# A two-layer hybrid trunk: gelu stores from ScalarE, key products ahead of the heads, a third gate buffer

## The chip, the cores and the metric

The kernel runs on one core of a Trainium2 chip. The metric is the time of one execution in microseconds of device time; of several runs the median counts. All arrays are float32, with batch 1, 1024 positions and a width of 1024.

## The reference

Only the first of the two layers is touched by the change. It computes, from `h = rmsnorm(x, norm_g[0])`:

```python
def mixer_ab(h, w_in, ..., glu_w, glu_b, w_out):
    proj = h @ w_in
    u_s5, g_s5, q, k, v, g_ret = jnp.split(proj, cuts, axis=-1)
    y_s5 = s5_mixer(u_s5, ..., glu_w, glu_b)           # ends with the two lines below
    #   y = jax.nn.gelu(y)
    #   y = y * jax.nn.sigmoid(y @ glu_w + glu_b)
    y_s5 = y_s5 * jax.nn.silu(g_s5)
    y_ret = retention(q, k, v) * jax.nn.silu(g_ret)    # q, k get rotary positions first
    return jnp.concatenate([y_s5, y_ret], axis=-1) @ w_out

def retention(q, k, v):            # 8 heads, 64 wide for q and k, 128 wide for v
    q = rope(q, positions) * (RET_DK ** -0.5)
    k = rope(k, positions)
    scores = einsum('bnihd,bnjhd->bnhij', qc, kc) * intra
    intra_out = einsum('bnhij,bnjhe->bnihe', scores, vc)
    ...                            # states carried from chunk to chunk, normalisation of each head
```

The second layer is a convolution module (projection, a causal convolution of width 31, layer norm, output projection), and a last rmsnorm ends the program.

## The kernel before

All activations lie transposed, features on the 128 partitions and the 1024 positions along the row, in two halves of 512. Every float32 product of the big projections is made as three matmuls (lines 269, 270 and 271, in `mm3`) of operands split into a high and a low part: `wh` and `wl` of the weights, `xh` and `xl` (or `yh` and `yl`, and so on) of the activations. A block of 128 output features is 2 halves x 8 input blocks x 3 = 48 matmuls of 128x512. `wnext` and `wload` bring the weights in a fixed sequence, two blocks ahead of the one in use: a DMA into `wf`, ScalarE's rounded copy `wh`, and the difference `wl` on GpSimd or VectorE (lines 260, 261).

The stages are, in the order of the program: the input projections with the state-space layer (`layer0_front`), the values and heads of the retention (`retention`), and the GLU, the output projection and the whole second layer (`layer0_back_and_layer1`).

The retention runs over four pairs of heads. For each pair `ret_proj` makes the key products (`mm_k`), evacuates them scaled (`kraw`, line 971), and rotates them: four DMAs (line 980) swap halves of partitions into `kswp`, GpSimd multiplies both by the rotary table (lines 984, 986), VectorE adds (line 987) and gives `krot`. Then the same is done for the queries (`mm_q`, `qraw`, `qswp`, `qrot`). `ret_proj` is a generator that yields once between the key products and the rest. Behind it come two calls of `y_pass` (lines 918 to 921), each of which loads one eighth of the state-space output (`yp`, a single buffer), takes the gelu on ScalarE (`yn`, a single buffer) and stores it to `yn_d`. From pair 1 on these follow the last square root of the pair before on ScalarE (`issue_after(self.last_rs.ins)`). Then `ret_heads` does the pair's heads:

- transposes of the keys (`ktp`, line 1077), scaled to `kt` (line 1079),
- the states: `kv` (line 1096) on TensorE and the running sum `S` on VectorE (line 1106),
- the scores `sp` from `krot` and `qrot` (line 1113), masked to `sc` (line 1119),
- the loads of the gates `grl` (line 1128),
- the outputs `ro` (lines 1140, 1145), their statistics on VectorE with a square root on ScalarE (line 540, `rs`), the normalised `on`,
- transposes back (`rt`, line 1168), the product with the gate in place, and the store to `yr_d` (line 1174).

The GLU that follows needs all of gelu(y): `load_split` reads `yn_d` (`yf`, line 1209) and splits it into `yh` and `yl` (lines 1178, 1180), and `mm_glu` sums over all eight blocks of it. Its products read the same operand buffers that hold the input of the query and key products until those are done.

All of the kernel's DMAs are issued by SyncE (SP). The instructions of each engine, SP's DMA issues among them, run in one fixed order. A planner makes that order when the program is built: an instruction that is emitted earlier has the higher priority, and the planner follows the program in a simulated time of its own, in which it takes, on each engine, the instruction of highest priority that is ready by then. `issue_after` and `chained` tie the order of single instructions. A tile with `bufs=n` has n buffers; the next use of a buffer waits for the last reader of the one before.

The key products of the next pair are thus already used as work between the steps of a pair's heads: they come behind the heads in priority, and are taken where the heads are not ready.

Of the kernel before, what the change touches and what calls it, by code (L numbers as in the profile page):

```python
# [11 lines left out]
F32 = mybir.dt.float32  # L12
# [7 lines left out]
P = 128  # L20
D = 1024
T = 1024
# [12 lines left out]
G0 = 3  # L35
TP = 6
LOWS = 18
P_ORDER = ([(1, nb) for nb in range(4)] + [(2, nb) for nb in range(4)] +
           [(i, nb) for i in (6, 7) for nb in range(4)] + [(4, nb) for nb in range(4)])

# [16 lines left out]
class Trunk:  # L57
# [22 lines left out]
    def plan(self):  # L80
# [11 lines left out]
        def wo(*names):  # L92
            return [(None, n) for n in names]

        def ab(h):
            return [q for nb in range(8) for q in ((A["w_c"][8 + nb], f"cb{nb}_{h}"),
                                                   (A["w_c"][nb], f"ca{nb}_{h}"))]
        def cg(h, nbs):
            return [(A["w_c"][16 + nb], f"cg{nb}_{h}") for nb in nbs]
        seq += wo(*(f"p{i}_{nb}" for i, nb in P_ORDER)) + wo("p5_0", "p3_0") + ab(0)  # L100
        seq += wo(*(f"p{i}_{nb}" for nb in range(1, 4) for i in (5, 3)))
# [812 lines left out]
    def y_pass(self, rp, cb):  # L914

        nc = self.nc
        yt = rp.tile([P, 8, P], F32, name=f"yp_{cb}", tag="yp", bufs=1)
        nc.sync.dma_start(yt[:], self.y_d[cb].rearrange("i h g m -> (h g) i m"))
        yn = rp.tile([P, P, 8], F32, name=f"yn_{cb}", tag="ynt", bufs=1)
        nc.scalar.activation(yn[:], yt[:].rearrange("p i m -> p m i"), AF.Gelu_apprx_tanh)  # L920
        nc.sync.dma_start(self.yn_d[cb * P:(cb + 1) * P], yn[:].rearrange("p m i -> p (m i)"))

    def retention(self, st):
        nc, A = self.nc, self.A
        r0 = self.r0 = self.pool("ret0", 1, stack=st)
        early = ExitStack()
        rq = self.rq = self.pool("retq", 1, stack=early, side="right")
        self.vt = [[(r0 if d else rq).tile([P, 4, HALF], F32, name=f"v{d}_{h}") for h in range(2)] for d in range(2)]
        self.rk = rq.tile([P, 2, T], F32, name="ropek")
        nc.sync.dma_start(self.rk[:], A["rope_k"])  # L930
        self.mask = r0.tile([P, NH, P], F32, name="retmask")
        nc.sync.dma_start(self.mask[:], A["ret_mask"])
        self.g128 = r0.tile([P, 4], F32, name="g128")
        nc.sync.dma_start(self.g128[:], A["ret_g128"])
        self.reps = r0.tile([P, NH], F32, name="reteps")
        nc.sync.dma_start(self.reps[:], A["ret_eps"])
        for pair in range(4):
            cur = list(self.ret_proj(pair))[-1]
            if pair == 0:
                with ExitStack() as vst:  # L940
                    V = self.ret_values(self.pool("vp", 1, stack=vst))
                self.rp = self.pool("ret", 1, stack=st)
                self.kdec = self.rp.tile([P, NH, 64], F32, name="kdec")
                nc.sync.dma_start(self.kdec[:], A["ret_kdec"])
                ry = self.pool("rety", 1, stack=early, side="right")
            with ExitStack() as held:
                if pair:
                    held.enter_context(self.tc.issue_after(self.last_rs.ins))
                for cb in (2 * pair, 2 * pair + 1):
                    self.y_pass(ry, cb)  # L950

            def turned():
                if pair == 3:
                    early.close()
                    self.lp = self.pool("l1", side="right")
            self.ret_heads(pair, *cur, V, turned)

    def ret_proj(self, pair):
# [45 lines left out]
    def ret_values(self, vp):  # L1004
# [28 lines left out]
        for n, i in enumerate(V_ORDER):  # L1033
# [29 lines left out]
            with self.tc.issue_after(self.last_sum.ins) if n > 1 else nullcontext():  # L1063
                for k in range(LOWS * (n - 1) // 6, LOWS * n // 6) if n else ():
                    self.weight_low(vp, k, (("wa", "wb"), ("wc", "wd")), 2)
        return lambda p, b, hh: vt[p // 2][b // 4][:, b % 4, (2 * (p % 2) + hh) * P:(2 * (p % 2) + hh + 1) * P]

    def ret_heads(self, pair, K, Q, qadds, V, turned):
        nc, rp = self.nc, self.rp
# [54 lines left out]
        gts = []  # L1124
        for hh in range(2):
            h = 2 * pair + hh
            gt = rp.tile([P, T], F32, name=f"grl_{h}", tag="grl", bufs=2)
            nc.sync.dma_start(gt[:], self.gr_d[h * P:(h + 1) * P])
            gts.append(gt)
        todo = []  # L1130
        for hf in range(2):
# [17 lines left out]
            for hh in range(2):  # L1149
                h, ps = 2 * pair + hh, pss[hh]  # L1150
# [21 lines left out]
        for hh in range(2):  # L1172
            h = 2 * pair + hh
# [8 lines left out]
    def layer0_back_and_layer1(self, st):  # L1182
# [34 lines left out]
        ys0, sg0, t2f, t3f = {}, {}, {}, {}  # L1217
        left = iter(range(LOWS, 32))

# [66 lines left out]
        def w_out_first():  # L1286
            nc.scalar.activation(self.warm[:], self.ones[:, 0:1], AF.Sqrt)
            yr0 = [operand(f"yr0{kb}", "A0", yr_load("yr0f", kb, 0)[:]) for kb in range(KB)]
            m1, u2, u3, t2, t3, t4 = {}, {}, {}, None, None, None
            for i, nb in P_ORDER:  # L1290
                if (i, nb) == (1, 2):
# [460 lines left out]
```

## Time and profile before

| | before |
|---|---|
| median of 3 runs | 1204.38 us (1200.94 to 1206.41) |
| the profiled execution | 1204.63 us |
| its span in the trace | 1202.9 us |
| mean granted TensorE clock | 0.991 |
| TensorE busy with matmuls | 1173.1 us, 98% |
| VectorE, GpSimd, ScalarE busy | 938.3, 688.5, 551.5 us |
| DMA | 271.19 MB, mean 225 GB/s |

The span is the time from the first to the last instruction of the trace. In the lines of the profile PE is TensorE, PEld its weight loads, DVE VectorE, ACT ScalarE, POOL GpSimd, SP SyncE; SPq stands for the issue of DMAs in SP's queue. `A<-B L980` says that tile A is written from B by line 980. An idle time in brackets, `[5.04 <-DVE qrot L987]`, stands ahead of the instruction and names what ended it. Matmuls overlap, so the length of one is longer than the distance to the next.

### The profile page before, as it was taken

Reading aid. Unit: us, or ns where it says so; the run is one execution under the profiler, and the core shown is the slowest. Engines: PE = TensorE matmul, PEld = TensorE weight load, DVE = VectorE, ACT = ScalarE, POOL = GpSimd, SP = SyncE. Lnnn points to the kernel's source line nnn. Section 1 sums busy time; section 2 is a strip of 40 time slices with the busy share of each in tenths; the row PEclk is TensorE's granted clock in tenths of the full one; section 3 lists DMA queues with packets and bytes.
Section 4 is the critical chain, followed back from the end, with each engine's and each line's share of the span. In section 5 each row is a group of like instructions: output and inputs, shape, how many; then the busy total and the mean of one; then the engine's idle time right before and its main releaser. Section 6 shows DMA issues by size and latency. Waiting matters only on the chain.

```text
span 1202.9 us, 17525 instructions
## 1 busy us (share of the span) xinstructions
PE 1173.1 (98%) x6150; PEld 972.4 (81%) x6150; DVE 938.3 (78%) x1529; ACT 551.5 (46%) x831; POOL 688.5 (57%) x489
## 2 busy tenths in 40 slices
PE   9999999999999999988899999999999999999997
PEld 7888888888888878876788788878887887888887
DVE  7865899999518777866878878379999999999643
ACT  7222333333125735323534535267755578444662
POOL 2059989888834224441444033338894578987642
PEclk9999999999999999989999999999999999999999
DMA  9362577788797786656888457866448653356873
GB/s 336 106 194 89 193 270 268 266 282 289 260 303 248 246 274 190 194 175 232 324 288 286 169 211 257 294 235 208 161 152 286 232 179 114 133 186 235 279 253 122
DMA packets 131480, 271.19 MB, mean 225 GB/s; under 512 B 12864, under 2 KB 41792, under 8 KB 131264
## 3 DMA queue, kind: packets, MB, share of 16 engines
q1 hardware_dynamic: 131392, 270.07, 65.8%
q8 instruction: 48, 0.79, 0.3%
q14 instruction: 40, 0.33, 0.1%
HBM read 194.07 MB, written 71.76 MB: 221 GB/s over the span
## 4 chain that ended last, share of the span: by engine, by line
PE 77%; DMA 8%; DVE 8%; issue 2%; POOL 2%; ACT 2%; SPq 1%; DVEq 0%; POOLq 0%; ACTq 0%
PE mm_g L271 7%; PE mm_g L270 7%; PE mm_g L269 6%; PE mm_w L269 4%; PE mm_w L270 4%; PE mm_w L271 4%; PE mm_oc L269 2%; PE mm_oc L270 2%; PE mm_oc L271 2%; PE mm_u L271 2%; PE mm_u L270 2%; PE mm_u L269 2%; PE mm_b L270 2%; PE mm_b L271 2%; PE mm_a L270 2%
## 5 line engine op out<-in xcount | busy, mean ns | idle before, releaser
L1441 DVE SCALAR_TENSOR_TENSOR cv<-u,convw,cv 128x512 f32<-128x512 f32 x358 | 245.2, 747 | 6.0 <-ACT cv L1427 4.3
L1421 POOL TENSOR_TENSOR tp<-tp,tp 128x512 f32<-128x512 f32 x104 | 138.7, 1336 | 33.4 <-ACT tp L1420 27.7
L270 PE MATMUL mm_g<-xl,wh_g 128*128 128x512 f32 x256 | 100.7, 393 | 0.0
L271 PE MATMUL mm_g<-xh,wl_g 128*128 128x512 f32 x256 | 100.7, 393 | 0.0
L269 PE MATMUL mm_g<-xh,wh_g 128*128 128x512 f32 x256 | 100.5, 393 | 0.0
L1420 ACT ACTIVATE tp<-u,convw 128x512 f32<-128x512 f32 x104 | 69.3, 714 | 9.2 <-POOL tp L1421 9.0
L270 PEld LDWEIGHTS mm_g<-xl,wh_g 128*128 128x128 f32 x256 | 48.1, 188 | 11.2 <-issue 1.4
L271 PEld LDWEIGHTS mm_g<-xh,wl_g 128*128 128x128 f32 x256 | 48.1, 188 | 10.4
L269 PEld LDWEIGHTS mm_g<-xh,wh_g 128*128 128x128 f32 x256 | 48.1, 188 | 9.7 <-issue 0.2
L269 PE MATMUL mm_oc<-zh,wh_woc 128*128 128x512 f32 (+1 forms) x152 | 54.5, 362 | 0.0
L271 PE MATMUL mm_oc<-zh,wl_woc 128*128 128x512 f32 (+1 forms) x152 | 54.4, 359 | 0.0
L270 PE MATMUL mm_oc<-zl,wh_woc 128*128 128x512 f32 (+1 forms) x152 | 54.2, 356 | 0.0
L271 PE MATMUL mm_g<-h1h,wl_cg 128*128 128x512 f32 x128 | 50.7, 396 | 1.1 <-POOL wl_cg L261 1.1
L270 PE MATMUL mm_u<-xl,wh_u 128*128 128x512 f32 x128 | 50.0, 391 | 0.9 <-DVE xl L383 0.9
L269 PE MATMUL mm_g<-h1h,wh_cg 128*128 128x512 f32 x128 | 50.9, 397 | 0.0
L269 PE MATMUL mm_glu<-yh,wh_glu 128*128 128x512 f32 x128 | 50.1, 393 | 0.7 <-ACT yh L1178 0.7
L270 PE MATMUL mm_b<-h1l,wh_cb 128*128 128x512 f32 x128 | 50.5, 394 | 0.2 <-DVE h1l L1358 0.2
L270 PE MATMUL mm_g<-h1l,wh_cg 128*128 128x512 f32 x128 | 50.5, 394 | 0.0
L271 PE MATMUL mm_a<-h1h,wl_ca 128*128 128x512 f32 x128 | 50.3, 393 | 0.0
L270 PE MATMUL mm_glu<-yl,wh_glu 128*128 128x512 f32 x128 | 50.1, 391 | 0.2 <-DVE yl L1180 0.2
L269 PE MATMUL mm_b<-h1h,wh_cb 128*128 128x512 f32 x128 | 49.9, 390 | 0.4 <-ACT h1h L1357 0.4
L269 PE MATMUL mm_a<-h1h,wh_ca 128*128 128x512 f32 x128 | 50.1, 392 | 0.0
(812 smaller groups left out, 3634.0 us busy)
## 6 DMA issues: line engine op xcount, KB each, us to landing
wf_g<-w_ab SPq DMA_DIRECT2D x16, 512.0 KB, 4.9
a<-w_out SPq DMA_DIRECT2D x32, 256.0 KB, 4.0
ws<-a SPq DMA_DIRECT2D x32, 256.0 KB, 4.3
lf<-w_c SPq DMA_DIRECT2D x32, 256.0 KB, 4.0
wf_p<-ws SPq DMA_DIRECT2D x16, 512.0 KB, 3.9
wf_cb<-w_c SPq DMA_DIRECT2D x16, 512.0 KB, 4.8
wf_ca<-w_c SPq DMA_DIRECT2D x16, 512.0 KB, 4.7
wl_cb<-lo_cb SPq DMA_DIRECT2D x16, 512.0 KB, 3.3
```

The lines of the kernel that those rows point to most:

```text
L269: nc.tensor.matmul(ps, wh[:, kb, :], xh, start=start, stop=False)
L270: nc.tensor.matmul(ps, wh[:, kb, :], xl, start=False, stop=False)
L271: self.last_mm = nc.tensor.matmul(ps, wl[:, kb, :], xh, start=False, stop=stop)
L1420: nc.scalar.mul(sk[:], u[:, k:k + HALF], cw[:, nb, k:k + 1])
L1421: gp.tensor_tensor(s0[:], s0[:], sk[:], op=ALU.add)
L1441: v.scalar_tensor_tensor(dst[:], *tap, accs_[i][:], op0=ALU.mult, op1=ALU.add)
```

## The change

Three edits in the retention. The DMA that stores gelu(y) is issued by ScalarE, which computed it, and no longer by SP. The key products of pair 1, 2 and 3 are emitted in front of the heads of pair 0, 1 and 2; the rotation of these keys, and the queries, stay behind those heads. The tag of the gates has three buffers, where it had two.

```diff
+AHEAD = (0, 1, 2)
...
         nc.scalar.activation(yn[:], yt[:].rearrange("p i m -> p m i"), AF.Gelu_apprx_tanh)
-        nc.sync.dma_start(self.yn_d[cb * P:(cb + 1) * P], yn[:].rearrange("p m i -> p (m i)"))
+        nc.scalar.dma_start(self.yn_d[cb * P:(cb + 1) * P], yn[:].rearrange("p m i -> p (m i)"))
...
+        ahead = None
         for pair in range(4):
-            cur = list(self.ret_proj(pair))[-1]
+            cur = list(ahead or self.ret_proj(pair))[-1]
...
+            ahead = pair in AHEAD and self.ret_proj(pair + 1)
+            if ahead:
+                next(ahead)
             self.ret_heads(pair, *cur, V, turned)
...
-            gt = rp.tile([P, T], F32, name=f"grl_{h}", tag="grl", bufs=2)
+            gt = rp.tile([P, T], F32, name=f"grl_{h}", tag="grl", bufs=3)
```

## Prediction

> **What bounds the kernel now.** I read the page's engine table first, then the table of stretches for the stage in which the change lies (425 to 600 us, the retention heads), then who waited for whom there, and last the engines' timelines around the two longest waits.
>
> ```profile
> span 1202.9 us, 17525 instructions
> PE 1173.1 (98%) x6150; PEld 972.4 (81%) x6150; DVE 938.3 (78%) x1529; ACT 551.5 (46%) x831; POOL 688.5 (57%) x489
> ```
>
> TensorE (PE) sets the time: it is busy for 1173.1 us of 1202.9. The change neither adds nor removes a matmul, so all it can win is PE's idle time, 29.8 us, and time in which PE ran at a reduced clock. The stretches (length; busy us of PE, PEld, DVE, ACT, POOL; PE clock; DMA share; GB/s) show where these lie:
>
> ```profile
> 495.00:525.00 30.00, 24.96 (x149) 20.86 (x149) 17.31 (x47) 6.96 (x6) 10.32 (x7) 0.94 0.69 207
> 525.00:540.00 15.00, 15.00 (x116) 12.98 (x115) 12.51 (x52) 5.64 (x10) 7.28 (x5) 0.89 0.28 72
> 560.00:580.00 20.00, 13.04 (x108) 9.93 (x106) 13.05 (x22) 7.65 (x11) 5.87 (x5) 0.99 0.85 318
> 580.00:595.00 15.00, 15.00 (x78) 12.89 (x75) 13.81 (x57) 8.15 (x12) 3.83 (x3) 0.90 0.92 346
> ```
>
> PE idles 30.00 - 24.96 = 5.04 us in pair 2 and 20.00 - 13.04 = 6.96 us in pair 3. Behind each gap 15 us run at a clock of 0.89 and 0.90, that is 15 x 0.11 = 1.65 and 15 x 0.10 = 1.5 us lost. Who ended PE's waits in this stage (total, times, longest), and the two waits of SP's queue that matter:
>
> ```profile
> PE sp L1113 <- DVE qrot L987: 8.0, 4, 5.0
> PE ro L1140 <- DVE sc L1119: 3.0, 2, 2.8
> PE mm_glu L269 <- ACT yh L1178: 0.7, 2, 0.4
> PE sp L1113 <- DVE S L1106: 0.6, 1, 0.6
> PE mm_glu L270 <- DVE yl L1180: 0.2, 1, 0.2
> SPq L921 <- ACT yn L920: 49.3, 8, 11.2
> SPq L1128 <- DMA yr_d<-grl: 13.6, 5, 5.5
> ```
>
> The score products sp wait for the rotated queries qrot; that is 8.0 of these 12.5 us. SP's queue stands 49.3 us at the stores of gelu(y) (L921) and 13.6 us at the loads of gates (L1128). Both are lines of the change.
>
> **Pair 2, the 5.04 us.** PE's timeline (start, length, line, product, count, idle before):
>
> ```profile
> 485.04 1.66 PE L1113 MATMUL sp<-qrot,krot 64*128 64x128 f32 x18 [0.45 <-DVE qrot L987]
> 506.79 0.39 PE L269 MATMUL mm_k<-xh,wh_k 128*128 128x512 f32 x1
> 517.76 1.75 PE L1096 MATMUL kv<-v,kt 128*64 128x128 f32 x28
> 524.55 2.47 PE L1113 MATMUL sp<-qrot,krot 64*128 64x128 f32 x18 [5.04 <-DVE qrot L987]
> 526.95 0.79 PE L270 MATMUL mm_k<-xl,wh_k 128*128 128x512 f32 x1
> 553.21 1.04 PE L1077 MATMUL ktp<-ident,krot 128*128 128x128 f32 x8
> ```
>
> The query products of pair 2 end where pair 3's key products begin, at 506.79. PE does 40 of those 48 products, then kv, and stands from 519.51 to 524.55 with eight key products and all of q3 ready behind sp in its fixed order. The chain it waits for:
>
> ```profile
> 506.99 0.69 DVE L971 TENSOR_TENSOR qraw<-mm_q,R 128x512 f32<-128x512 f32 x1 [2.00 <-PE mm_q L271]
> 508.24 2.09 ACT L920 ACTIVATE yn<-yp 128x1024 f32<-128x1024 f32 x1 [5.56 <-DMA yp<-y_d]
> 510.36 0.33 SPq L921 DMA_DIRECT2D yn_d<-yn  x1
> 510.79 0.38 SPq L918 DMA_DIRECT2D yp<-y_d  x1
> 511.26 2.26 SPq L980 DMA_DIRECT2D qswp<-qraw  x3
> 513.62 1.02 SPq L1174 DMA_DIRECT2D yr_d<-grl  x2
> 514.69 1.32 SPq L980 DMA_DIRECT2D qswp<-qraw  x1
> 512.63 1.36 DVE L1079 TENSOR_TENSOR kt<-ktp,kdec 128x512 f32<-128x512 f32 x2 [1.46 <-PE ktp L1077]
> 521.38 2.48 POOL L986 TENSOR_TENSOR qswp<-qswp,ropek 128x512 f32<-128x512 f32 x2 [7.63 <-DMA qswp<-qraw]
> 522.67 2.33 DVE L987 TENSOR_TENSOR qrot<-qrot,qswp 128x512 f32<-128x512 f32 x2 [7.75 <-POOL qswp L986]
> ```
>
> qraw is done at 507.68, but the four swap copies start only at 511.26: on SP a store of gelu stands ahead of them that waits for ACT until 510.33. That costs 511.26 - 507.68 = 3.58 us, and two yr stores ahead of the fourth swap another 1.02.
>
> - *Stores on ScalarE.* The 3.58 us go, if the next yp load (which needs the single yp tile that the same gelu reads, and so waits for the same 510.33) no longer stands ahead of the swaps. I think that it will not: with pair 2's key products ahead of pair 1's heads, those heads run later against the q2 products, their last square root too, and both gelus of the pair are issued behind that. The planner then sees the swaps ready before the load. qrot, which let sp start at 524.55, would come at about 524.5 - 3.6 = 520.9.
> - *Key products in front.* The eight k3 products left move in front of kv and sp. The first 40 took 517.76 - 506.79 = 10.97 us, in which two groups of eight transposes (rt, ktp) lie, 2 x 1.04 by the row of pair 3's: 8.89 / 40 = 0.22 each, 1.8 for eight. sp is then wanted at 519.5 + 1.8 = 521.3, after 520.9: the wait is 0.
> - *Clock.* Without the gap the 18 score products take 1.66 as in pair 1, not 2.47: 0.81. The stretch's 1.65 is the upper bound; I take the row, 0.81.
>
> Pair 2: 5.04 + 0.81 = 5.85 us gained; bounds 0 (nothing moves) and 6.69. Pair 1 goes with it: its 0.45 us in the row at 485.04 is covered by the remaining k2 products, which now come first. Pair 0 has its key products of pair 1 done before its heads already: 0.
>
> **Pair 3, the 6.96 us.** Here no key products follow, and the cover is GLU products, whose operands are the stored gelu:
>
> ```profile
> 548.25 0.39 PE L269 MATMUL mm_glu<-yh,wh_glu 128*128 128x512 f32 x1
> 562.20 1.16 PE L1113 MATMUL sp<-qrot,krot 64*128 64x128 f32 x16 [1.25 <-DVE qrot L987]
> 579.19 1.69 PE L1140 MATMUL ro<-S,qrot 64*128 64x128 f32 x14 [2.77 <-DVE sc L1119]
> 543.40 2.08 ACT L920 ACTIVATE yn<-yp 128x1024 f32<-128x1024 f32 x1
> 548.45 0.69 DVE L971 TENSOR_TENSOR qraw<-mm_q,R 128x512 f32<-128x512 f32 x1 [0.44 <-PE mm_q L271]
> 552.85 0.32 SPq L921 DMA_DIRECT2D yn_d<-yn  x1
> 553.21 2.82 SPq L980 DMA_DIRECT2D qswp<-qraw  x4
> 557.17 0.87 SPq L1174 DMA_DIRECT2D yr_d<-grl  x2
> 563.15 0.32 SPq L1128 DMA_DIRECT2D grl<-gr_d  x1
> 563.56 0.86 SPq L1209 DMA_DIRECT2D yf<-yn_d  x2
> ```
>
> - *Stores.* The last store (552.85) has no yp load behind it, so here the swaps are freed for certain: qraw is done at 549.14, the swaps start at 553.21, 4.07 us later. Of the 8.0 us of qrot waits 8.0 - 5.04 - 0.45 = 2.51 are pair 3's; they go.
> - *Third gate buffer.* SP stands from 558.04 to 563.15 because the first gate load needs the buffer that a yr store is still reading, and the yf loads, GLU's last operands, stand behind it. With three buffers gate 6 takes the one of gate 3, free since pair 1; gate 7 takes that of gate 4 and still waits for the store issued at 557.17. So 0 to 5.1 us for yf; the 0.7 + 0.2 us that GLU waits for yh and yl go.
> - *What stays.* The waits on S and sc (0.6 + 3.0), which DVE's order makes. Of the 1.5 us of clock I take half, 0.75.
> - *What comes back.* q3 ends about 5.85 + 0.45 = 6.3 us earlier, but the gelus of pair 3 are tied to pair 2's last square root, and sp of pair 2 moves only from 524.55 to 521.3 and by the 0.45, 3.7 us. PE reaches the end of its cover 2.6 us earlier against its operands; the third buffer may hide all of it or none. I take half, 1.3.
>
> Pair 3: 2.51 + 0.9 + 0.75 - 1.3 = 2.86 us gained; bounds a loss of 2.6 (nothing gained, all given back) and a gain of 6.96 + 1.5 = 8.46.
>
> **ScalarE's own cost.** Eight issues at 0.32 us (552.85) are 2.6 us of an engine that is 46% busy. Behind a store on ACT stand casts of weights and of yh and the table load for the next square roots, 0.3 us later each; no row of before shows a store on ACT. Bounds 0 and 8 x 0.32 = 2.6 us; I take 0, since the store directly follows its gelu there and waits for nothing else. The planner also lays out everything behind anew: 0, within 3 us either way, about what is idle after 595 us in one of the long stretches:
>
> ```profile
> 595.00:680.00 85.00, 83.22 (x365) 68.45 (x364) 67.96 (x80) 37.57 (x60) 31.82 (x18) 0.98 0.74 252
> ```
>
> (1.78 us of idle and 85 x 0.02 = 1.7 us of clock.)
>
> Sum: 5.85 + 0.45 + 2.86 = 9.16. The profiled execution took 1204.63 us (span 1202.9 and 1.7 around it), the median of the runs shown is 1204.38, 0.25 less: 1204.63 - 9.16 - 0.25 = 1195.2 us.
>
> A rule speaks against the first edit. The Trainium skill, page "DMA: Bandwidth & Descriptors", section "Issuing engines are not separate DMA queues", says that starting transfers from several engines saves only the sequencer time that it takes to start them. By that rule the stores give SP back 8 x 0.32 = 2.6 us, none of it PE's. The 49.3 us that SP's queue stands at these stores are a wait and not issue time, and the rule has no term for it.
>
> **Rivals.** *The wait changes its name.* SP keeps the yp load ahead of the swaps, and since it waits for the same gelu, the swaps start as late as before. For it: in the trace the load follows each store directly (510.36, 510.79). Against it: the later heads. The later heads also bring that gelu later, so the wait is no shorter, though the eight key products come in front: the 5.04 us stay, and 0.45 + 2.86 are won: 1204.38 - 3.31 = 1201.1 us. The rule above gives this time too.
>
> *The cover runs out (slower).* Key products in front hold up each pair's heads; in pair 2 by 1.8 us for the products, and, since the transposes ktp now come behind k3, by 1.04 of ktp and the 1.36 of kt on DVE that follows, 4.2 in all. The gelus of pair 3, hence GLU's last operands, come 4.2 us later, while q3 is not later. PE, which has nothing else at that place, idles 4.2 us more and then runs slow for 1.65, and GLU's tail on DVE is pushed into a second gap of the size of the present 0.6: 4.2 + 1.65 + 0.6 = 6.45, so 1204.38 + 6.45 = 1210.8 us. It decides when the gelus of pair 3 start later than now (543.40) while q3 ends earlier than 548.25. Against it: the third buffer frees the yf loads.
>
> **How the numbers follow.** Forecast 0.48, wait renamed 0.27, cover runs out 0.25. A measurement tells 0.5% here, 6.0 us: faster is under 1198.4, slower over 1210.4. Of the forecast's 0.48, 0.07 falls in the band; of the renamed wait's 0.27, 0.06 falls below and 0.03 above it; of the last 0.25, 0.09 in the band. Faster 0.41 + 0.06 = 0.47, same 0.07 + 0.18 + 0.09 = 0.34, slower 0.03 + 0.16 = 0.19. The lowest sum of bounds is 1204.4 - 6.69 - 0.45 - 8.46 = 1188.8; with a part of the 3 us of the new layout 1187. Upwards the range takes in the slower case and 1.2 us of the new layout: 1212. The forecast's own range is 1189 to 1199.
>
> **What would show it.** Right: sp of pair 2 waits under 1 us; the swap copies start within 1 us of qraw in pairs 2 and 3; PE's idle time in the stage falls from 13 us to about 5; the clock near 0.97 there. Renamed wait: SP's queue has near 49 us at the yp load (L918) instead of L921, and sp of pair 2 still waits 4 us or more. Cover run out: PE's waits are for yh and yl, over 4 us, and pair 3's gelus start later than 543. Wrong altogether: PE's idle time in the stage as before and the difference elsewhere, after 600 us.

## The result and the profile after

The changed kernel took 1197.43 us (median; 1194.84 to 1199.91) against 1204.37 for the kernel before beside it: a ratio of 0.9946, 95% interval 0.9922 to 0.9971. It is faster by 6.9 us, where 9.2 were forecast. The number is near; the way to it was only partly the forecast one. The profiled execution of the changed kernel is the slowest of its five (1199.91 us), so it and the one of before (1204.63) are only 4.7 us apart, and what the traces place is 4.7 us and not 6.9.

The engine table of the kernel after:

```profile
span 1198.1 us, 17522 instructions
PE 1167.2 (97%) x6150; PEld 967.8 (81%) x6150; DVE 941.0 (79%) x1529; ACT 554.3 (46%) x833; POOL 687.4 (57%) x489
```

PE was busy for 5.9 us less with the same 6150 matmuls, at a mean granted clock of 0.995, where it was 0.991; its idle time is 1198.1 - 1167.2 = 30.9 us, where it was 29.8. In this pair of traces the gain is thus one of clock and not of idle time. The page also has a new DMA queue, q10, with the 4.19 MB of gelu(y) that ScalarE now sends.

The stretches of the retention stage in the kernel after, in the columns of those shown of before:

```profile
495.00:525.00 30.00, 29.93 (x188) 25.18 (x186) 22.16 (x68) 11.04 (x13) 14.98 (x10) 1.00 0.49 154
525.00:540.00 15.00, 9.20 (x83) 7.96 (x84) 8.49 (x19) 2.51 (x3) 3.33 (x3) 0.80 0.63 198
560.00:580.00 20.00, 16.62 (x126) 14.01 (x127) 12.96 (x27) 8.61 (x13) 2.02 (x2) 1.00 0.92 321
580.00:595.00 15.00, 13.86 (x65) 11.01 (x63) 12.27 (x50) 11.48 (x16) 5.61 (x3) 1.00 1.04 383
```

The gap of pair 2 has left the first row (29.93 of 30.00 busy, it was 24.96) and stands in the second: 5.80 us idle, and a clock of 0.80. PE's waits in the stage (425 to 600 us), all of them, and two of SP's:

```profile
PE sp L1118 <- DVE S L1111: 5.2, 1, 5.2
PE rt L1173 <- DVE on L1165: 2.6, 2, 1.7
PE mm_glu L270 <- ACT yh L1183: 2.2, 1, 2.2
PE ro L1145 <- DVE sc L1124: 1.8, 1, 1.8
PE kv L1101 <- DVE kt L1084: 1.7, 2, 1.0
SPq L919 <- ACT yn L921: 29.0, 7, 13.4
SPq L1133 <- DMA yr_d<-grl: 9.8, 3, 5.3
```

No wait for qrot is left; in before they were 8.0 us. But these five sum to 13.5 us, where all waits of before came to 13.2 (the 12.5 us of the rows that the prediction shows, and 0.7 that kv waited for kt): a wait for the running sum S has taken the place of the one for qrot. SP's 49.3 us at the stores are gone, and 29.0 us of waiting for the same gelus now stand at the yp loads (L919).

To see where the time went, the span can be cut at the last matmul of five products (`mm_v`, `mm_glu`, `mm_w`, `mm_a`, `mm_oc`), each read from the view of its tile. One profiled execution each, us:

| | to the last mm_v | retention and GLU | output projection | layer 1, projection | to the last mm_oc |
|---|---|---|---|---|---|
| before | 436.7 | 222.6 | 45.6 | 316.2 | 169.8 |
| after | 438.6 | 220.5 | 41.9 | 314.9 | 170.3 |

The stage that was changed gave 2.1 us. The output projection behind it, in which no line was changed, gave 3.7. The first and the fourth column differ by +1.9 and -1.3 us though no edit touches work there, and two kernels of the experiments that leave the retention as it was in before (b_wl, b_yr) take 223.6 and 221.3 us for retention and GLU. So the 2.1 us are no larger than such differences; the 3.7 are (the projection takes 44.2 to 47.9 us in seven of the fourteen kernels of this document, 41.9 to 42.2 in the other seven).

**The new wait.** Timelines of the kernel after, of PE, DVE, ACT and SP around it (start, length):

```profile
518.87 1.03 PE L1082 MATMUL ktp<-ident,krot 128*128 128x128 f32 x8
525.58 1.75 PE L1101 MATMUL kv<-v,kt 128*64 128x128 f32 x28 [0.65 <-DVE kt L1084]
527.26 1.38 PE L1118 MATMUL sp<-qrot,krot 64*128 64x128 f32 x18
537.03 1.83 PE L1118 MATMUL sp<-qrot,krot 64*128 64x128 f32 x13 [5.22 <-DVE S L1111]
518.56 4.58 DVE L992 TENSOR_TENSOR qrot<-qrot,qswp 128x512 f32<-128x512 f32 x2 [5.13 <-POOL qswp L991]
528.77 0.73 DVE L1111 SCALAR_TENSOR_TENSOR S<-S,g,kv 128x128 f32<-128x128 f32 x2
535.93 0.69 DVE L1185 TENSOR_TENSOR yl<-yf,yh 128x512 fp32r<-128x512 f32 x1 [6.44 <-ACT yh L1183]
536.54 0.34 DVE L1111 SCALAR_TENSOR_TENSOR S<-S,g,kv 128x128 f32<-128x128 f32 x1
535.28 1.23 ACT L1183 CAST yh<-yf 128x512 fp32r<-128x512 f32 x2 [12.19 <-DMA yf<-yn_d]
523.76 0.92 SPq L1179 DMA_DIRECT2D yr_d<-grl  x2
526.84 2.42 SPq L985 DMA_DIRECT2D kswp<-kraw  x4
529.94 1.02 SPq L1214 DMA_DIRECT2D yf<-yn_d  x2
```

The scores go straight on from kv at 527.26: qrot had been there since 523.14. Then the sums S stop. DVE's order has two of them, then a low part yl of GLU's operands, then the other four, with a second yl among them. The yl need yh, yh needs the load yf, and SP issues yf only at 529.94, behind the yr stores, which waited, and the swaps of the next keys. So DVE stands 6.44 us at a step that nobody needs before GLU, with S behind it, and PE stands 5.22. (The scores do not read S. In the kernel they take their banks from the pool, `ps_aux`, that kv's come from, and a bank comes free once the sums have read the kv in it.)

**The output projection.** Before (the first three rows: a stretch and timelines of PE and DVE) and after (the last two):

```profile
655.00:685.00 30.00, 28.22 (x118) 22.84 (x117) 25.65 (x37) 19.12 (x32) 3.45 (x2) 0.94 0.55 187
667.34 0.50 PE L271 MATMUL mm_w<-ysh,wl_p 128*128 128x512 f32 x1 [1.78 <-DVE wl_p L165]
666.08 1.21 DVE L165 TENSOR_TENSOR wl_p<-wf_p,wh_p 128x1024 fp32r<-128x1024 f32 x1
```

```profile
655.00:685.00 30.00, 30.00 (x134) 24.86 (x133) 27.50 (x39) 18.76 (x31) 1.62 (x1) 1.00 0.51 165
659.51 1.22 DVE L166 TENSOR_TENSOR wl_p<-wf_p,wh_p 128x1024 fp32r<-128x1024 f32 x1
```

In before the low part of the second block of weights (wl_p) comes at 667.29, PE waits 1.78 us for it, and the stretch runs at a mean clock of 0.94, 30 x 0.06 = 1.8 us: together 3.6 of the 3.7 that the table shows. In after VectorE makes it 6.6 us earlier, PE is busy for the whole stretch, and the clock is 1.00.

### The profile page after: what moved, and what is told of

Read it like the earlier page. It is cut to its first block, busy times and chain, and to the rows that moved or that the text cites. A ratio compares the mean times of both kernels' runs of the same rounds, so it can differ in the third digit from the quotient of the medians.

```text
span 1198.1 us, 17522 instructions
## 1 busy us (share of the span) xinstructions
PE 1167.2 (97%) x6150; PEld 967.8 (81%) x6150; DVE 941.0 (79%) x1529; ACT 554.3 (46%) x833; POOL 687.4 (57%) x489
## 3 DMA queue, kind: packets, MB, share of 16 engines
q10 hardware_dynamic: 1152, 4.19, 0.9%
## 4 chain that ended last, share of the span: by engine, by line
PE 79%; DMA 8%; DVE 7%; POOL 2%; ACT 2%; issue 2%; SPq 1%; DVEq 0%; POOLq 0%; ACTq 0%
PE mm_g L272 7%; PE mm_g L271 7%; PE mm_g L270 6%; PE mm_w L270 3%; PE mm_w L271 3%; PE mm_w L272 3%; PE mm_u L272 2%; PE mm_u L271 2%; PE mm_oc L272 2%; PE mm_oc L270 2%; PE mm_oc L271 2%; PE mm_u L270 2%; PE mm_b L271 2%; PE mm_a L271 2%; PE mm_b L272 2%; PE mm_a L270 2%
## 5 line engine op out<-in xcount | busy, mean ns | idle before, releaser
L165 ACT CAST wh_p<-wf_p 128x1024 fp32r<-128x1024 f32 x28 | 29.5, 1054 | 46.2 <-PE mm_w L271 37.6
L270 PE MATMUL mm_u<-xh,wh_u 128*128 128x512 f32 x128 | 49.2, 395 | 1.7 <-ACT wh_u L261 1.7
```

Source lines behind the costliest of these rows:

```text
L165: self.nc.scalar.copy(wh[:].rearrange(fl), wf[:])
L270: nc.tensor.matmul(ps, wh[:, kb, :], xh, start=start, stop=False)
```

## Experiments

The ratios are to the kernel before, run beside each kernel; it had medians of 1206.64 us (the first four kernels) and 1206.13 us (all later ones). The whole change is shown with the ratio of the result. The stages are from one profiled execution each.

**One edit at a time.** The changed kernel with the other edits undone:

```diff
 s_only, sk:          nc.scalar.dma_start(self.yn_d[...], yn[...])    (k_only, g_only: nc.sync)
 k_only, sk:          AHEAD = (0, 1, 2)                               (s_only, g_only: AHEAD = ())
 g_only:              tag="grl", bufs=3                               (the others: bufs=2)
```

> The stores on ScalarE alone (no key products in front, two gate buffers). Theory A (the key products took pair 2's query wait away; the store alone only renames the wait): SP stands at the yp load (L919 or near) in place of the store, the swaps of pair 2 still start 3 us or more behind qraw, sp of pair 2 waits 4 us or more, time 1201 to 1205. Theory B (the stores did it, as the prediction's first step has it): sp of pair 2 waits under 1.5 us, time under 1200.

> The key products in front alone (stores by SP, two gate buffers). Theory A: the swaps of pair 2 start within 2 us of qraw though SP still issues the stores, sp of pair 2 does not wait for qrot, time 1197 to 1201. Theory B: the swaps stand behind the store as before, sp waits 3 us or more, time 1202 or more.

> The third gate buffer alone. Both theories: pair 2 as before (sp waits about 5 us); the 5 us for which SP stands at a gate load in pair 3 go or shrink, and GLU's waits for yh and yl (0.9 us) with them. Time 1201 to 1204.5, that is a gain of 0 to 3 us.

> Stores and key products, two gate buffers. If the third buffer carries nothing (theory A: the gain is the key products'): within 1.5 us of the whole change, 1196 to 1199. If it carries a part, as the prediction has it (0 to 5 us of GLU's operands): 1200 or more, with SP standing at gate loads and waits for yh in pair 3 over 3 us.

| | median us | ratio, 95% interval | retention and GLU | output projection |
|---|---|---|---|---|
| before | | | 222.6 | 45.6 |
| stores alone (s_only) | 1203.43 | 0.9968 (0.9950 to 0.9986) | 223.9 | 45.3 |
| keys alone (k_only) | 1198.85 | 0.9938 (0.9917 to 0.9959) | 220.7 | 41.9 |
| gates alone (g_only) | 1207.73 | 1.0011 (0.9994 to 1.0028) | 225.0 | 44.8 |
| stores and keys (sk) | 1201.61 | 0.9951 (0.9932 to 0.9970) | 222.6 | 42.2 |
| the whole change | 1197.43 | 0.9946 (0.9922 to 0.9971) | 220.5 | 41.9 |

The key products alone bring the gain; with the two other edits on top of them the intervals overlap. The third gate buffer alone gives nothing that can be measured, where 0 to 3 us were expected: GLU's waits for yh and yl are gone, as expected, but in the same trace the outputs ro wait 5.0 us for sc, where they waited 3.0. The time of sk, 1201.61 us, is that of the case in which the third buffer carries a part; the signs of that case are not there (the waits for yh are 2.7 us, SP's at the gates 8.2, in the whole change 9.8), and the intervals with and without it overlap. The stores alone win 0.3%, which the profile does not place: their stage is 1.3 us longer than before in this pair of traces.

Stores alone, PE's and SP's waits in the stage, and the timelines of SP, DVE and PE in pair 2:

```profile
PE sp L1118 <- DVE qrot L992: 9.7, 4, 5.0
SPq L919 <- ACT yn L921: 32.8, 7, 11.4
506.66 0.69 DVE L976 TENSOR_TENSOR qraw<-mm_q,R 128x512 f32<-128x512 f32 x1 [2.00 <-PE mm_q L272]
502.38 7.81 SPq L919 DMA_DIRECT2D yp<-y_d  x2
510.28 2.66 SPq L985 DMA_DIRECT2D qswp<-qraw  x3
524.22 2.47 PE L1118 MATMUL sp<-qrot,krot 64*128 64x128 f32 x18 [5.03 <-DVE qrot L992]
```

This is the prediction's rival "the wait changes its name", for this edit by itself: no store stands on SP any more, but the yp load waits there for the same gelu, the swaps start 2.9 us after qraw is done (507.35), and the scores wait 5.03 us, where it was 5.04. The Trainium skill, page "DMA: Bandwidth & Descriptors", section "Issuing engines are not separate DMA queues", by which another issuing engine saves only issue time, agrees with what pair 2 shows.

Pair 3 is no different. With the stores alone its swaps start at 552.69, 3.0 us after qraw (549.65), behind four yf loads that wait for stores of gelu(y); the waits for qrot in all pairs are 9.7 us, more than the 8.0 of before. With the key products alone they start at 554.71, directly behind qraw (554.68).

Keys alone, the same two views:

```profile
PE sp L1118 <- DVE S L1111: 6.7, 1, 6.7
SPq L922 <- ACT yn L921: 40.4, 7, 11.4
508.82 0.32 SPq L922 DMA_DIRECT2D yn_d<-yn  x1
509.71 2.87 SPq L985 DMA_DIRECT2D qswp<-qraw  x4
```

SP still issues the stores and stands 40.4 us at them, and yet qrot is waited for no more: the key products removed that wait without the stores' edit. The swaps of pair 2 start 2.3 us after qraw (507.39), where under 2 were expected. The key products also bring the wait for S: 6.7 here, 6.9 with the stores as well, 5.2 in the whole change, and none over 0.7 in a kernel without them.

**Is the wait for S what the new order puts in front?** Two kernels hold the low parts yl of GLU's blocks 4 and 5 back on VectorE until pair 2's scores have been masked: the whole change (hold), and the keys alone (k_hold).

```diff
+        if pair == 2:                       # in ret_heads, behind the masks
+            self.mid2 = self.masked[1]
...
-    self.split(f, a, b, v, None if halves or h == 0 else ...)
+    self.split(f, a, b, v, (self.mid2 if kb in (4, 5) else None) if halves or h == 0 else ...)
```

> The whole change, and the two splits yl of blocks 4 and 5 tied on VectorE behind pair 2's last masked scores; nothing else is changed. Theory A (the qrot wait of pair 2 was turned into a wait for S behind these splits, and it is paid): sp of pair 2 no longer waits for S (5.2 us in the whole change), the clock behind it stays 1.00, and the time falls by 4 to 7 us against the whole change, to 1190 to 1194 where that has 1197.4. Theory C (PE has its cover back later: GLU's operands set the end of this stage): the wait for S goes, waits for yh and yl in pair 3 grow by the same 5 us, and the time stays within 2 us of the whole change.

> Key products in front and the tied splits, stores by SP, two gate buffers. If stores and third buffer are worth nothing: within 1.5 us of the whole change with the tied splits. If they matter once the wait for S is gone (the pair 3 part of the prediction, 2 to 3 us): slower than that by 2 us or more.

Measured: hold 1197.95 us, 0.9933 (0.9910 to 0.9957); k_hold 1196.23, 0.9929 (0.9903 to 0.9955). Hold's stretches, and all its waits of PE in the stage over 1 us:

```profile
525.00:540.00 15.00, 15.00 (x144) 13.08 (x139) 12.63 (x37) 3.03 (x5) 7.15 (x5) 1.00 0.58 174
540.00:560.00 20.00, 12.22 (x73) 9.62 (x73) 14.29 (x45) 7.70 (x9) 4.75 (x3) 0.84 0.53 170
PE mm_glu L270 <- ACT yh L1185: 4.1, 1, 4.1
PE rt L1175 <- DVE on L1167: 3.1, 1, 3.1
PE mm_glu L270 <- ACT sg L1243: 1.8, 1, 1.8
```

That settles the cause of the wait for S: it is the low parts in front of it, and with them held back it is gone in both kernels. The gap of 525 to 540 is gone, and the last query product of pair 3 comes 8.1 us earlier (540.3, after: 548.4). But 540 to 560 then holds 7.78 us of idle time at a clock of 0.84: PE reaches the GLU products before their last operands. The stage is 1.2 us shorter than in after (219.3 and 220.5), and the times can't be told apart. Most of the 5.2 us were thus not on the path that sets the end; they stood ahead of a wait for GLU's operands. k_hold (218.3 us) is no slower than hold, though it has neither the stores' edit nor the third buffer: these two gave nothing here either.

**The output projection alone.** Two versions of the kernel before take away the cause that its trace names: wl of that block on GpSimd (b_wl), and VectorE's differences of the retention's result held behind that wl (b_yr).

```diff
 b_wl:
-    return self.wload_split(..., name, self.nc.vector)
+    return self.wload_split(..., name, self.nc.gpsimd if name == "p1_1" else self.nc.vector)
 b_yr:
+    if name == "p1_1":                      # in wload_split; low is the subtraction that makes wl
+        self.low11 = low
...
-    v.tensor_tensor(f[:], f[:], t2f[kb][:], op=ALU.subtract)
+    with self.tc.issue_after(self.low11.ins):
+        v.tensor_tensor(f[:], f[:], t2f[kb][:], op=ALU.subtract)
```

> The kernel before with one instruction moved: the low part of the weight block p1_1 of the output projection is made on GpSimd and not on VectorE. Theory A (3.5 us of the change's gain lie in the output projection, where PE of before waits 1.8 us for this block on VectorE and then runs slow): the wait goes, the stretch from the last GLU product to the last projection product falls from 45.6 us to about 42, time 2.5 to 4 us under before. Rival D (VectorE is simply late there, the next block waits instead): the stretch stays above 44.5, time within 1.5 us of before.

> The kernel before with one order tied: on VectorE the differences yr0g - t2f (operands of the last projection products) stand behind the low part of weight block p1_1, which PE needs first. Theory A (3.5 us of the change's gain are this block's lateness on VectorE): PE's wait for wl_p (1.8 us) goes and the slow clock behind it, the stretch from the last GLU product to the last projection product falls from 45.6 us to 42 to 43, time 2 to 4 us under before. Rival D (the stretch is bound otherwise, the next block waits instead): the stretch stays above 44.5 and the time within 1.5 us of before.

Measured: b_wl 1205.65 us, 1.0004 (0.9987 to 1.0022); b_yr 1204.67, 0.9985 (0.9965 to 1.0004). The timelines (b_wl's POOL row and its wait of PE; b_yr's wait):

```profile
666.27 2.79 POOL L165 TENSOR_TENSOR wl_p<-wf_p,wh_p 128x1024 fp32r<-128x1024 f32 x1
PE mm_w L271 <- POOL wl_p L165: 2.7, 1, 2.7
```

```profile
673.51 0.80 PE L273 MATMUL mm_w<-ysh,wl_p 128*128 128x512 f32 x1 [2.06 <-DVE wl_p L165]
```

Neither shortens the stretch (46.7 and 47.9 us): GpSimd makes the block no earlier than VectorE did and takes 2.79 us, and in b_yr the next block is the one that is late. The place is right, but it is not one late instruction: the weights as a whole run late there.

What goes with it in every trace is ScalarE. It makes the rounded copy wh_p of that second block, which wl_p needs; in these two traces that copy stands behind all eight copies of the retention's results (yr00h to yr07h). Before and after:

```profile
660.80 1.04 ACT L164 CAST wh_p<-wf_p 128x1024 fp32r<-128x1024 f32 x1
656.02 1.05 ACT L165 CAST wh_p<-wf_p 128x1024 fp32r<-128x1024 f32 x1
```

The last GLU product ends at 659.3 in before and at 659.1 in after. So the copy starts 1.5 us behind it in the one and 3.1 us ahead of it in the other. In all seven kernels with a long projection (44.2 to 47.9 us; b_wl and b_yr are among them) it starts 0.6 to 4.0 us behind the last GLU product, and in the seven with a short one from 4.1 us ahead to 0.2 behind. No run changes this alone, so it is seen together and not shown as the cause.

**A second yp buffer.** It was to let the yp load go without waiting for the gelu, so that the swaps of pair 2 come free: with the stores alone (s_yp2) and on top of the whole change (yp2).

```diff
-  tag="yp", bufs=1
+  tag="yp", bufs=2
```

> Stores on ScalarE and a second yp buffer, no key products in front, two gate buffers. If the yp load that waits for the same gelu is what holds the swaps back (the prediction's rival): the swaps of pair 2 start within 1.5 us of qraw and sp of pair 2 waits under 2.5 us instead of 5.0, time 2 to 5 us under stores alone, 1199 to 1202 on the scale where stores alone had 1203.4. If something else holds them: sp still waits 4 us or more and the time is that of stores alone.

> The whole change with a second yp buffer. Theory C (pair 3 is bound by the last operands of the GLU, which come by load of yp, gelu, store, load of yf, split, one behind another): the load of the last yp block comes one gelu earlier, the waits for yh in pair 3 go, and the time falls by 3 to 5 us against the whole change, to 1192.5 to 1194.5. Theory A (the wait for S in pair 2 costs its 5.2 us and the clock, and nothing else is bound there): the wait for S stays, and the time is within 2 us of the whole change.

Measured: s_yp2 1196.45 us, 0.9929 (0.9903 to 0.9956); yp2 1202.44, 0.9963 (0.9942 to 0.9984). SP's timeline of s_yp2, PE's wait in it, and all waits of yp2 over 1.5 us from 425 to 690:

```profile
501.83 8.22 SPq L919 DMA_DIRECT2D yp<-y_d  x2
523.67 2.47 PE L1118 MATMUL sp<-qrot,krot 64*128 64x128 f32 x18 [5.04 <-DVE qrot L992]
```

```profile
PE sp L1118 <- DVE S L1111: 5.0, 1, 5.0
PE mm_glu L270 <- ACT yh L1183: 4.3, 1, 4.3
PE mm_w L272 <- DVE wl_p L166: 3.0, 2, 1.6
```

Both missed what was expected of the mechanism. In s_yp2 the planner only issues the loads one block further ahead, so the load of the block after next waits for that gelu, and the swaps start at 510.14, with the stores alone at 510.28. It gains nevertheless: retention and GLU take 219.0 us, 223.9 with the stores alone, and its interval and that of s_only overlap only from 0.9950 to 0.9956. A part of it lies in pair 3: from 540 to 595 us PE idles 5.1 us at a clock of 1.00, where it idled 6.4 at clocks of 1.00, 0.91 and 0.89; why is not tested. On top of the whole change the same buffer wins nothing (either case that was expected had a lower time): the wait for S stays, the yh wait is 4.3 us, and the output projection is back at 45.5 us with waits for wl_p, although the key products stand in front.

**Together.** The whole change with the second yp buffer, the held low parts and the held differences (best), and the same without the key products and with two gate buffers (sy_yr; no held low parts):

> The whole change, a second yp buffer, the splits yl of blocks 4 and 5 behind pair 2's masked scores, and the tied order of the weight block p1_1. If the wait for S was only given back to GLU's operands (theory C), taking away both gives the sum: 5 to 9 us under the whole change, 1188 to 1192. If another wait takes their place (the normalised outputs ahead of rt, 3.1 us in the kernel with the tied splits): 1193 to 1196.

> No key products in front: the stores on ScalarE, a second yp buffer, two gate buffers, and the tied order of the weight block p1_1. If the key products give only what these give by other means: 1193 to 1195 (the 1196.5 of stores and second yp buffer, less the 1.7 us that PE waits there for wl_p and some clock). If the key products have a gain of their own in pair 2: 1196 or more, with sp of pair 2 still waiting 5 us, and above the kernel with everything by 5 us.

Measured: best 1195.00 us, 0.9899 (0.9872 to 0.9925); sy_yr 1197.18, 0.9918 (0.9886 to 0.9949). Best's waits of PE over 1 us from 425 to 690, all of them:

```profile
PE mm_glu L272 <- ACT yh L1187: 4.0, 1, 4.0
PE rt L1177 <- DVE on L1169: 3.2, 1, 3.2
```

This version beats the kernel before clearly. Its ratio is 0.5% below that of the changed kernel (0.9899 and 0.9946), but the two intervals overlap by 0.0003, and those of s_yp2, hold and k_hold overlap with it too. It is the case that was expected if another wait takes the place of the others. Its retention and GLU take 217.2 us, its output projection 41.9. The wait for S and those for wl_p are gone; the one for GLU's operands is what remains. sy_yr, which keeps a wait of 4.5 us for qrot, is 0.9918 without any key product in front: 218.7 and 42.0 us. So the key products are one way to this time and not the only one, and best is 2.2 us under it, where 5 were expected if they had a gain of their own. In it the held differences do shorten the projection (44.2 in s_yp2), which they did not in before.

## Why the prediction was right or wrong

*Direction and size.* Faster, as forecast; 6.9 us of 9.2. The steps that make up the sum did less well than the sum.

*Pair 2, 5.85 us: the wait went, the gain did not.* The 5.04 us for qrot are gone, but 5.22 for S stand in the same pair, at a clock of 0.80. The step that failed is that the wait becomes 0 and the clock comes back with it, and behind it the term "What stays": it took the wait on S as before (0.6 us, measured 5.2), and looked for what is late next only among the scores' own operands. Moving the heads behind more products moved the sums too, into a part of DVE's order where low parts for GLU already stood.

*How the wait for qrot went.* By cover, not by the stores. From the end of qraw to that of qrot it takes 523.14 - 507.96 = 15.2 us in after and 525.00 - 507.68 = 17.3 in before, 2.1 less: the swaps follow the first gelu of the pair now and not the second, in k_only too, where SP issues the store. But the scores were wanted at 527.26 instead of 519.51. The prediction's cover held eight key products, 1.8 us; in the trace, between ktp (518.87) and kv (525.58), there are also 22 of pair 3's query products, which it had left behind the scores. So "stores on ScalarE, 3.58 us" was put down to the wrong edit, with the right side thought: that later heads bring the swaps ahead of a load.

*Pair 1 and pair 3.* The 0.45 and the 2.51 us of qrot waits are gone, but not by the stores: the prediction said of pair 3 that there "the swaps are freed for certain", and with the stores alone they still start 3.0 us after qraw and qrot is still waited for. With the key products alone both waits are gone. In the whole change pair 3's idle time did not fall, 7.1 us from 540 to 595 and 7.0 before; what was gained is the clock, which from 560 to 595 was 0.99 and 0.90 and is 1.00. The waits for yh did not go but grew from 0.7 to 2.2, waits of 2.6 for the normalised outputs came, and sc fell from 3.0 to 1.8. "What comes back" was the right term, too small at 1.3. What goes with it is in ACT's timelines, the first gelu of pair 3 in before, in after and in hold:

```profile
543.40 2.08 ACT L920 ACTIVATE yn<-yp 128x1024 f32<-128x1024 f32 x1
550.58 2.06 ACT L921 ACTIVATE yn<-yp 128x1024 f32<-128x1024 f32 x1
546.21 1.99 ACT L921 ACTIVATE yn<-yp 128x1024 f32<-128x1024 f32 x1
```

It starts later in both, as the rival "the cover runs out" said, by 7.2 and 2.8 us. In hold, where the queries also end earlier, that rival's sign is there, a wait for yh of 4.1 us, but at a time that is still below before's.

*Third gate buffer, 0 to 5.1 us in pair 3.* 0: nothing measurable alone. SP's wait at the gates fell from 13.6 to 9.8 us in after, but that is not the buffer's doing: with two buffers it is 7.8 in s_only and k_only and 8.2 in sk. And GLU's wait for yh grew all the same. Alone, the buffer did take away the 0.9 us for yh and yl, as the prediction had it, and the wait for sc grew by 2.0.

*ScalarE's own cost.* 0 fits what was measured: the stores alone cost no time. An issue took 0.33 to 0.40 us there. ACT's busy time rose by 2.8 us in after, but the profile does not count issues as busy: two more table loads of 1.28 us are in it, which s_only, with the same eight stores, does not have.

*The layout behind, "0, within 3 us".* It gave 3.7 us, more than the stage that was changed. The forecast had named the sign for it: idle time in the stage as before (13.2 us, 13.5 after) and the difference after 600. That sign is there, so the number was met in good part from a place that the prediction had set to zero: that it came out near is luck. Of the profiled 4.7 us, 2.1 come from the stage and 3.7 from the projection; the front and the rest sum to 1.1 the other way.

*What stays open.* Which single thing makes the projection's weights come in time. The short stretch goes with the key products in k_only, sk and every held version; but yp2 has them and is long, and sy_yr lacks them and is short. How VectorE and ScalarE come out of the GLU decides it as a whole; the start of ScalarE's copy wh_p goes with it in all fourteen traces, but that is argued from these cases, and no run isolates it. Nor is the 0.3% of the stores alone located, nor what the second yp buffer wins with them and loses with the key products.

## What to carry to other kernels

When work is moved to cover a wait, follow every in-order engine through the new order, not only the chain of the wait: here a step for a later stage, waiting for its load, came to stand ahead of sums that were needed at once. Removing a stall is worth no more than the time until the next operand that is late anyway; in hold the queries ended 8.1 us earlier, and the stage became 1.2 us shorter. And look for the result behind the stage that was edited too, since with a planned order every later stage is laid out anew.

## What the runs showed of the hardware

In these traces a gap slows what follows it: the 13 score products behind the gap of 5.22 us took 1.83 us, the same 13 in pair 1 of that trace 1.04, and 11 products ro behind them 1.87 instead of 0.94. It need not be that long: behind the gap of 1.78 us in the projection of before, the granted clock was 0.63 from 667.34 to 672. The same subtraction of 128x1024 took 1.21 us on VectorE in before and 2.79 on GpSimd in b_wl. And two adds of the rotation, pair 2's queries, took 4.58 us on VectorE in after, where they took 2.33 in before. GpSimd was busy for 3.79 of these 4.58 us and for 1.19 of the 2.33, and two such adds at 507.87 in after, with GpSimd idle throughout, took 1.28. So they were slow where GpSimd worked beside them; no run tests it.
